# Index add on one core: one more staged batch, larger pieces for the copies, masks built on VectorE

## The chip, the cores and the metric

The kernel runs on one core of one Trainium2 chip. The metric is device time in microseconds (us) for one execution. Times are medians of several runs; the profile is of one execution, and its span (first to last instruction) is a little shorter than that execution's time.

## The reference

`x` has 32 batches of 512 rows of 256 floats. Every batch has 128 updates: an index (a row of this batch) and a source row of 256 floats. An index can occur several times in a batch.

```python
result = x.copy()
for b in range(32):
    for i in range(128):
        result[b, indices[b, i]] += source[b, i]
```

`x` and the result have 16.8 MB each, the source 4.2 MB.

## The kernel before

The kernel is a direct program: every instruction, semaphore and wait is written out, and each engine works through its own list in the order of the text. No planner moves anything.

There are two ways for a batch to reach the output.

**Direct batches** (26 of 32). The batch is copied from `x` to the output within DRAM (`copy`, L99, 512 KB, in rows of 4 KB). Beside this, the 128 rows that its updates name are gathered from `x` into a tile `got` by an indirect DMA of GpSimd (`gather`, L341). TensorE multiplies a 128 x 128 mask `same` (update i and update j have the same index) with the source rows, so that every update gets the sum of all updates to its row (L266). VectorE adds this to the gathered rows, for two batches at once (L278). An indirect DMA then scatters the rows over the copy (`scatter`, L359). Of several updates to one row only one may be written: VectorE multiplies `same` with the mask `before` and takes a maximum, and where an earlier update names the same row, the row number in `to_i` is pushed past the end, so that the transfer leaves this row out (L230 to L250). From the ninth direct batch on, the gather uses `to_i` as well and leaves these rows out too; the first eight use `row_i`, which is ready sooner.

**Staged batches** (`STAGED`, 6 of 32). The whole batch is loaded into SBUF (`load_x`, L112), 4 rows for each partition. VectorE compares the 512 row numbers in `place_f` with each update's index and so makes a mask `onehot` (L287), TensorE multiplies it with the source rows (L302), VectorE adds the result to the batch in two halves (L312), and SP stores it (L383).

The order around the change:

- SP issues, in one queue (q1 in the profile): the indices, the source for groups of four batches, the copies of batches 4 to 31, the loads of staged batches, and at the end the stores, each behind a wait for its last addition. ACT issues the copies of batches 0 to 3 in a queue of its own (q10), then clears some `got` tiles.
- GpSimd makes the constants (L129 to L157), waits for the row numbers, then issues all gathers and after them all scatters (q0). A gather with `to_i` waits for that group's masks. A scatter waits for its batch's copy, its sum and its masks.
- VectorE makes the row numbers and `place_f`, then the masks of groups 0 to 3. After that, for each group g: the sums of group g, the masks of group g + 4, and a staged batch of group g - 2 if there is one. The last staged batch comes at the end. TensorE follows the same order.

The loop that fixes this order:

```python
for g in range(NG):
    sums(g)
    if g + MASKS_AHEAD < NG:
        pe_broadcast(g + MASKS_AHEAD)
        dve_masks(g + MASKS_AHEAD)
    waiting += [b for b in STAGED if b // GB == g - 2]
    if waiting:
        staged_batch(waiting.pop(0))
```

Of the kernel before, what the change touches and what calls it, by code (L numbers as in the profile page):

```python
# [7 lines left out]
P = 128  # L8


GB = 4
COPY_DESC = 4096
STAGED = (7, 11, 15, 19, 23, 27)
MASKS_AHEAD = 4
SKIP_FROM = 8

# [2 lines left out]
def kernel(  # L19
# [13 lines left out]
    B, S, D = x.shape  # L33
    _, NU = indices.shape
    CH = S // P
    assert NU == P and S % P == 0 and B % GB == 0
    NG = B // GB
    DIRECT = [b for b in range(B) if b not in STAGED]
    N_DIRECT = len(DIRECT)
    assert N_DIRECT % 2 == 0  # L40

    f32 = mybir.dt.float32
    i32 = mybir.dt.int32
    Alu = mybir.AluOpType
# [5 lines left out]
    sb = ctx.enter_context(tc.tile_pool(name="sb", bufs=1))  # L50
# [3 lines left out]
    idx_bt = sb.tile([B, NU], f32)  # L54
    ident = sb.tile([B, B], f32)
    base = sb.tile([P, B], i32)
    before = sb.tile([P, GB, P], f32)
    place = sb.tile([P, CH, P], i32)
    place_f = sb.tile([P, CH, P], f32)
    idx_f = sb.tile([P, B], f32)  # L60
    base_f = sb.tile([P, B], f32)
    row_f = sb.tile([P, B], f32)
    row_i = sb.tile([P, B], i32)
    dup = sb.tile([P, B], f32)
    to_i = sb.tile([P, B], i32)
    src = [sb.tile([P, GB, D], f32, name=f"src{g}") for g in range(NG)]
    got = [sb.tile([P, 2, D], f32, name=f"got{h}") for h in range(N_DIRECT // 2)]
    same = [sb.tile([P, GB, P], f32, name=f"same{g}") for g in range(NG)]
    earlier = [sb.tile([P, GB, P], f32, name=f"earlier{k}") for k in range(2)]
    staged = {b: sb.tile([P, CH, D], f32, name=f"staged{b}") for b in STAGED}  # L70
    onehot = {b: sb.tile([P, CH, P], f32, name=f"onehot{b}") for b in STAGED}
    N_ADD, N_SP = 3, 2
    idx_ps = pp.tile([P, B], f32, space=PSUM)
    bc = [pp.tile([P, GB, P], f32, space=PSUM, name=f"bc{k}") for k in range(2)]
    add = [pp.tile([P, 2, D], f32, space=PSUM, name=f"add{k}") for k in range(N_ADD)]
# [5 lines left out]
    s_got = {b: tc.alloc_semaphore(f"s_got{b}") for b in DIRECT}  # L81
    s_in = {b: tc.alloc_semaphore(f"s_in{b}") for b in STAGED}
    s_out = tc.alloc_semaphore("s_out")
    s_store = tc.alloc_semaphore("s_store")
    sems = {n: tc.alloc_semaphore(f"s_{n}") for n in ("pool", "dve", "pe", "act")}
    done = dict.fromkeys(sems, 0)

    def mark(name, ins):
        ins.then_inc(sems[name], 1)
        done[name] += 1  # L90
        return done[name]

    V, T, G = nc.vector, nc.tensor, nc.gpsimd

    with tc.tile_critical(no_gpsimd_drain=True):  # L95
# [2 lines left out]

        def copy(b):  # L99
            (nc.scalar if b < GB else nc.sync).dma_start(  # L100
                out=out[b].rearrange("(p c) d -> p (c d)", p=P),
                in_=x[b].rearrange("(p c) d -> p (c d)", p=P),
                max_dma_last_dim=COPY_DESC,
            ).then_inc(s_copy[b], 16)

        def load_src(g):
# [5 lines left out]
        def load_x(b):  # L112
            nc.sync.dma_start(  # L113
                out=staged[b][:, :, :], in_=x[b].rearrange("(j c) d -> j c d", c=CH)
            ).then_inc(s_in[b], 16)
# [3 lines left out]
        for g in range(NG):  # L119
            if g + 2 < NG:  # L120
                load_src(g + 2)
            for b in range(g * GB, (g + 1) * GB):
                if b in DIRECT:
                    copy(b)
                if b % GB == 1 and g * GB - 1 in STAGED:
                    load_x(g * GB - 1)


        m = mark("pool", G.memset(ident[:, :], 0.0))  # L129
# [4 lines left out]
                out=ident[:, :], in_=ident[:, :], compare_op=Alu.not_equal, fill=1.0,  # L134
                base=0, pattern=[[-1, B]], channel_multiplier=1,
# [2 lines left out]
        k_const = mark(  # L138
            "pool", G.iota(out=base[:, :], pattern=[[S, B]], base=0, channel_multiplier=0)  # L139
        )  # L140

        k_place = mark(
            "pool",
            G.iota(
                out=place[:, :, :], pattern=[[1, CH], [CH, P]], base=0, channel_multiplier=0
            ),
        )

        m = mark("pool", G.memset(before[:, :, :], 1.0))
        G.wait_ge(sems["pool"], m)  # L150
        k_before = mark(
            "pool",
            G.affine_select(  # L153
                out=before[:, :, :], in_=before[:, :, :], compare_op=Alu.is_gt, fill=0.0,
                base=0, pattern=[[0, GB], [-1, P]], channel_multiplier=1,
            ),
        )  # L157


        for h in range(SKIP_FROM // 2, N_DIRECT // 2):  # L160
            k_zero = mark("act", nc.scalar.memzero(got[h][:, :, :]))  # L161


        V.wait_ge(sems["pool"], k_const)
        mark("dve", V.tensor_copy(out=base_f[:, :], in_=base[:, :]))  # L165
        V.wait_ge(s_idx, 16)
        k = mark(
            "dve",
# [1 line left out]
                out=idx_bt[:, :],  # L170
                in_=idx_raw[:, :].rearrange("b (u w) -> b u w", w=2)[:, :, 0],
# [5 lines left out]
        V.wait_ge(sems["pe"], k)  # L177
        k_rows = mark(
            "dve",
            V.tensor_tensor(out=row_i[:, :], in0=idx_ps[:, :], in1=base_f[:, :], op=Alu.add),  # L180
        )
        m = mark("dve", V.tensor_copy(out=idx_f[:, :], in_=idx_ps[:, :]))
        V.wait_ge(sems["dve"], m)
        mark(
            "dve",
            V.tensor_tensor(out=row_f[:, :], in0=idx_f[:, :], in1=base_f[:, :], op=Alu.add),
        )
        V.wait_ge(sems["pool"], k_place)
        m = mark("dve", V.tensor_copy(out=place_f[:, :, :], in_=place[:, :, :]))
        V.wait_ge(sems["dve"], m)  # L190

        k_bc, k_same, k_to, k_sum, k_hot, k_spread = {}, {}, {}, {}, {}, {}
        k_staged = {}

# [17 lines left out]
        def dve_masks(g):  # L212

            gs = slice(g * GB, (g + 1) * GB)
            V.wait_ge(sems["pe"], k_bc[g])
            k_same[g] = mark(
                "dve",
                V.tensor_tensor(  # L218
                    out=same[g][:, :, :],
                    in0=bc[g % 2][:, :, :],  # L220
                    in1=idx_f[:, gs].unsqueeze(2).to_broadcast([P, GB, P]),
                    op=Alu.is_equal,
                ),
            )
            if g == 0:
                V.wait_ge(sems["pool"], k_before)
            V.wait_ge(sems["dve"], k_same[g])
            m = mark(
                "dve",
                V.tensor_tensor(  # L230
                    out=earlier[g % 2][:, :, :], in0=same[g][:, :, :],
                    in1=before[:, :, :], op=Alu.mult,
                ),
            )
            V.wait_ge(sems["dve"], m)
            m = mark(
                "dve",
                V.tensor_reduce(  # L238
                    out=dup[:, gs], in_=earlier[g % 2][:, :, :], op=Alu.max,
                    axis=mybir.AxisListType.X,  # L240
                ),
            )
            V.wait_ge(sems["dve"], m)

            k_to[g] = mark(
                "dve",
                V.scalar_tensor_tensor(  # L247
                    out=to_i[:, gs], in0=dup[:, gs], scalar=float(2 * B * S),
                    in1=row_f[:, gs], op0=Alu.mult, op1=Alu.add,
                ),  # L250
            )

        def sums(g):

            T.wait_ge(s_src[g], 16)
            T.wait_ge(sems["dve"], k_same[g])
            for b in range(g * GB, (g + 1) * GB):
                if b in STAGED:
                    continue
                n = DIRECT.index(b)  # L260
                h = n // 2
                if n % 2 == 0 and h >= N_ADD:
                    T.wait_ge(sems["dve"], k_sum[h - N_ADD])
                k = mark(
                    "pe",
                    T.matmul(  # L266
                        out=add[h % N_ADD][:, n % 2, :], lhsT=same[g][:, b % GB, :],
                        rhs=src[g][:, b % GB, :], start=True, stop=True,
                    ),
                )  # L270
                if n % 2 == 0:
                    continue
                V.wait_ge(sems["pe"], k)
                V.wait_ge(s_got[DIRECT[n - 1]], 16)
                V.wait_ge(s_got[b], 16)  # L275
                k_sum[h] = mark(
                    "dve",
                    V.tensor_tensor(  # L278
                        out=got[h][:, :, :], in0=got[h][:, :, :],
                        in1=add[h % N_ADD][:, :, :], op=Alu.add,  # L280
                    ),
                )

# [40 lines left out]
        for g in range(MASKS_AHEAD):  # L324
            pe_broadcast(g)
            dve_masks(g)
        waiting = []
# [8 lines that stand above are left out]
# [45 lines left out]
        for b in STAGED:  # L381
            nc.sync.wait_ge(sems["dve"], k_staged[b])
            nc.sync.dma_start(  # L383
                out=out[b].rearrange("(j c) d -> j c d", c=CH), in_=staged[b][:, :, :]
# [34 lines left out]
```

## Time and profile before

| | |
|---|---|
| runs | median 83.69 us (83.33 to 83.92, 3 runs) |
| profiled execution | 83.13 us, span 81.4 us |
| busy share of the span | PE 54%, DVE (VectorE) 47%, ACT 7%, POOL (GpSimd) 67% |
| moved by DMA | 30.33 MB, mean 373 GB/s |
| indirect transfers | 26 gathers, 26 scatters, 1.0 us of POOL each |
| granted TensorE clock | 0.816 of full speed |

A busy digit of 9 in a slice means 90% or more of that fortieth of the span. The queue table has packets, MB, and the time that their packets took as a share of 16 engines over the span; shares of one stretch can add up to more than 1, since records of an engine's packets overlap. "us to landing" is from a transfer's issue until its data have arrived. In the timeline a line has the start, the length, the engine, the line of the kernel, the operation with its tiles, and in brackets the idle time before it and what ended that.

### The profile page before, as it was taken

The numbers are of one execution on the slowest core, as the hardware profiler recorded it, in microseconds if no ns is written. First come the engines' busy times: TensorE is split into PE (matmuls) and PEld (weight loads), VectorE is DVE, ScalarE is ACT, GpSimd is POOL, SyncE is SP. The second block draws the span as 40 slices with busy tenths as digits, with TensorE's granted clock in tenths as the row PEclk, the third lists the DMA queues.
The fourth block names the chain that finished last, engine by engine and source line by source line (L and its number), as shares of the span: only waits on it lengthen the run. The fifth ranks groups of instructions, "written<-read, shape, count | busy, mean of one in ns | idle before, by whom it ended". The sixth has DMA issues, their size and how long they took to land.

```text
span 81.4 us, 653 instructions
## 1 busy us (share of the span) xinstructions
PE 44.2 (54%) x165; PEld 34.8 (43%) x165; DVE 38.1 (47%) x69; ACT 6.1 (7%) x10; POOL 54.5 (67%) x62
## 2 busy tenths in 40 slices
PE   0299999999870099939494007993591900000000
PEld 0299986877540078638282006781460700000000
DVE  1749999999799903653700291009408006000000
ACT  0299700000000000000000000000000000000000
POOL 4668777877878787878777787877878687740000
PEclk9999999999999755599999985559858998555555
DMA  0899999999999999999999999999999999999930
GB/s 0 282 275 387 385 380 390 361 416 416 397 397 417 414 392 417 419 415 387 405 408 418 394 416 418 420 414 418 416 415 421 386 423 418 417 416 418 385 133 0
DMA packets 12243, 30.33 MB, mean 373 GB/s; under 512 B 1584, under 2 KB 5725, under 8 KB 12240
## 3 DMA queue, kind: packets, MB, share of 16 engines
q1 hardware_dynamic: 9168, 22.06, 69.5%
q0 software_dynamic: 2496, 6.15, 19.5%
q10 hardware_dynamic: 576, 2.10, 6.6%
q8 instruction: 1, 0.02, 0.1%
q14 instruction: 2, 0.02, 0.0%
HBM read 24.41 MB, written 20.19 MB: 548 GB/s over the span
## 4 chain that ended last, share of the span: by engine, by line
SPq 47%; DMA 18%; issue 10%; POOL 9%; DVE 2%; POOLq 2%; DVEq 0%
SPq L100 30%; DMA staged<-in_x_dram 18%; SPq L107 10%; POOL out_dram L363 9%; SPq L113 6%; POOLq L378 2%; DVE staged L312 1%; DVE got L278 1%; SPq L97 0%; DVEq L275 0%; SPq L414 0%; DVEq L308 0%; SPq L95 0%
## 5 line engine op out<-in xcount | busy, mean ns | idle before, releaser
L363 POOL DMA_INDIRECT out_dram<-got,to_i x26 | 25.7, 987 | 7.9 <-issue 7.0
L302 PE MATMUL spread<-src,onehot 128*128 128x256 f32 x48 | 16.8, 512 | 16.9 <-DVE onehot L287 14.6
L349 POOL DMA_INDIRECT got<-in_x_dram,to_i x18 | 18.2, 1012 | 5.5 <-issue 3.4
L302 PEld LDWEIGHTS spread<-src,onehot 128*128 128x128 f32 x48 | 11.6, 254 | 21.4 <-issue 19.4
L312 DVE TENSOR_TENSOR staged<-staged,spread 128x512 f32<-128x512 f32 x12 | 7.8, 684 | 25.4 <-DMA staged<-in_x_dram 16.5
L266 PE MATMUL add<-src,same 128*128 128x256 f32 x52 | 16.7, 469 | 0.4 <-DVE got L278 0.4
L266 PEld LDWEIGHTS add<-src,same 128*128 128x128 f32 x52 | 12.3, 245 | 3.6 <-DVE got L278 0.8
L203 PE MATMUL bc<-idx_bt,ident 32*128 32x128 f32 x64 | 11.9, 354 | 0.0
L203 PEld LDWEIGHTS bc<-idx_bt,ident 32*128 32x128 f32 x64 | 10.9, 256 | 1.4 <-DVE earlier L230 0.3
L349 POOL DMA_INDIRECT got<-in_x_dram,row_i x8 | 8.4, 1047 | 3.1 <-issue 1.8
L278 DVE TENSOR_TENSOR got<-got,add 128x512 f32<-128x512 f32 x13 | 8.6, 683 | 1.3 <-PE add L266 0.9
L218 DVE TENSOR_TENSOR same<-bc,idx_f 128x512 f32<-128x512 f32 x8 | 5.5, 684 | 1.1 <-PE bc L203 1.1
L230 DVE TENSOR_TENSOR earlier<-same,before 128x512 f32<-128x512 f32 x8 | 5.5, 692 | 0.3
L238 DVE TENSOR_REDUCE dup<-earlier 128x4 f32<-128x512 f32 x8 | 5.5, 686 | 0.3
L161 ACT ACTIVATE got<-got 128x512 uint32<-128x512 uint32 x9 | 4.8, 615 | 0.0
L287 DVE TENSOR_SCALAR onehot<-place_f,idx_f 128x512 f32<-128x512 f32 x6 | 2.9, 487 | 0.0
L176 PE MATMUL idx_ps<-ident,idx_bt 32*128 32x32 f32 x1 | 0.3, 280 | 3.6 <-DVE idx_bt L169 3.6
L165 DVE CAST base_f<-base 128x32 f32<-128x32 int32 x1 | 1.0, 993 | 1.7 <-POOL base L139 1.7
L176 PEld LDWEIGHTS idx_ps<-ident,idx_bt 32*128 32x128 f32 x1 | 0.2, 178 | 3.6 <-POOL before L153 3.6
L161 ACT ACT_TABLE_LOAD x1 | 1.3, 1283 | 3.6 <-issue 3.6
L247 DVE SCALAR_TENSOR_TENSOR to_i<-dup,row_f 128x4 int32<-128x4 f32 x8 | 1.3, 162 | 0.3
L169 DVE CAST idx_bt<-idx_raw 32x128 f32<-32x128 int32 x1 | 0.7, 687 | 0.1
(14 smaller groups left out, 3.6 us busy)
## 6 DMA issues: line engine op xcount, KB each, us to landing
out_dram<-in_x_dram SPq DMA_DIRECT2D x22, 512.0 KB, 15.0
src<-in_source_dram SPq DMA_DIRECT2D x8, 512.0 KB, 13.8
staged<-in_x_dram SPq DMA_DIRECT2D x6, 512.0 KB, 15.1
out_dram<-staged SPq DMA_DIRECT2D x6, 512.0 KB, 17.6
out_dram<-in_x_dram ACTq DMA_DIRECT2D x4, 512.0 KB, 7.9
out_dram<-got,to_i POOLq DMA_INDIRECT x26, 5.8
got<-in_x_dram,to_i POOLq DMA_INDIRECT x18, 5.9
got<-in_x_dram,row_i POOLq DMA_INDIRECT x8, 6.3
```

Source lines behind the costliest of these rows:

```text
L100: (nc.scalar if b < GB else nc.sync).dma_start(out=out[b].rearrange("(p c) d -> p (c d)", p=P), in_=x[b].rearrange("(p c) d -> p (c d)", p=P),
L107: nc.sync.dma_start(out=src[g][:, :, :], in_=source[g * GB : (g + 1) * GB].rearrange("e u d -> u e d"),).then_inc(s_src[g], 16)
L161: k_zero = mark("act", nc.scalar.memzero(got[h][:, :, :]))
L203: T.matmul(out=bc[g % 2][:, e, :], lhsT=ident[:, b : b + 1].to_broadcast([B, P]), rhs=idx_bt[:, :], start=True, stop=True,),
L218: V.tensor_tensor(out=same[g][:, :, :], in0=bc[g % 2][:, :, :], in1=idx_f[:, gs].unsqueeze(2).to_broadcast([P, GB, P]), op=Alu.is_equal,),
L230: V.tensor_tensor(out=earlier[g % 2][:, :, :], in0=same[g][:, :, :], in1=before[:, :, :], op=Alu.mult,),
L266: T.matmul(out=add[h % N_ADD][:, n % 2, :], lhsT=same[g][:, b % GB, :], rhs=src[g][:, b % GB, :], start=True, stop=True,),
L278: V.tensor_tensor(out=got[h][:, :, :], in0=got[h][:, :, :], in1=add[h % N_ADD][:, :, :], op=Alu.add,),
L302: T.matmul(out=spread[n % N_SP][:, c, :], lhsT=onehot[b][:, 2 * half + c, :], rhs=src[b // GB][:, b % GB, :], start=True, stop=True,),
L312: V.tensor_tensor(out=rows, in0=rows, in1=spread[n % N_SP][:, :, :], op=Alu.add),
L349: G.indirect_dma_start(out=got[n // 2][:, n % 2, :], out_offset=None, in_=x_rows, in_offset=bass.IndirectOffsetOnAxis(ap=(to_i if skips el ...
L363: G.indirect_dma_start(out=out_rows, out_offset=bass.IndirectOffsetOnAxis(ap=to_i[:, b : b + 1], axis=0), in_=got[n // 2][:, n % 2, :], in ...
```

## The change

Batch 3 becomes a staged batch as well, so 25 direct batches stay. Since their number is now odd, the last is summed by itself. The copies within DRAM are described as 32 rows of 16 KB instead of 128 rows of 4 KB. GpSimd no longer makes the wide constants `place` and `before`; it makes a row of counts, `column` (128 wide), and a column of counts, `update`. VectorE makes `before` (now 128 x 128) by one comparison and `place_f` by four operations out of these. The mask product reads `before` repeated for the four batches of a group. `base_f` goes: the additions read the integer `base`.

```diff
-COPY_DESC = 4096
-STAGED = (7, 11, 15, 19, 23, 27)
+COPY_ROWS = 32
+STAGED = (3, 7, 11, 15, 19, 23, 27)
...
-                out=out[b].rearrange("(p c) d -> p (c d)", p=P),
-                in_=x[b].rearrange("(p c) d -> p (c d)", p=P),
-                max_dma_last_dim=COPY_DESC,
+                out=out[b].rearrange("(p c) d -> p (c d)", p=COPY_ROWS),
+                in_=x[b].rearrange("(p c) d -> p (c d)", p=COPY_ROWS),
+                max_dma_last_dim=4 * S * D // COPY_ROWS,
...
-        k_place = mark(
-            "pool",
-            G.iota(
-                out=place[:, :, :], pattern=[[1, CH], [CH, P]], base=0, channel_multiplier=0
-            ),
-        )
-
-        m = mark("pool", G.memset(before[:, :, :], 1.0))
-        G.wait_ge(sems["pool"], m)
-        k_before = mark(
-            "pool",
-            G.affine_select(
-                out=before[:, :, :], in_=before[:, :, :], compare_op=Alu.is_gt, fill=0.0,
-                base=0, pattern=[[0, GB], [-1, P]], channel_multiplier=1,
-            ),
-        )
+        mark(
+            "pool", G.iota(out=update[:, :], pattern=[[0, 1]], base=0, channel_multiplier=1)
+        )
+        k_column = mark(
+            "pool", G.iota(out=column[:, :], pattern=[[1, P]], base=0, channel_multiplier=0)
+        )
...
-        mark("dve", V.tensor_copy(out=base_f[:, :], in_=base[:, :]))
...
-        V.wait_ge(sems["pool"], k_place)
-        m = mark("dve", V.tensor_copy(out=place_f[:, :, :], in_=place[:, :, :]))
+        V.wait_ge(sems["pool"], k_column)
+        m = mark("dve", V.tensor_copy(out=update_f[:, :], in_=update[:, :]))
         V.wait_ge(sems["dve"], m)
+        mark(
+            "dve",
+            V.tensor_scalar(
+                out=before[:, :], in0=column[:, :], scalar1=update_f[:, :], scalar2=None,
+                op0=Alu.is_lt,
+            ),
+        )
+        for c in range(CH):
+            k_place = mark(
+                "dve",
+                V.tensor_scalar(
+                    out=place_f[:, c, :], in0=column[:, :], scalar1=float(CH),
+                    scalar2=float(c), op0=Alu.mult, op1=Alu.add,
+                ),
+            )
...
-            if g == 0:
-                V.wait_ge(sems["pool"], k_before)
-            V.wait_ge(sems["dve"], k_same[g])
+            V.wait_ge(sems["dve"], max(k_same[g], k_place))
...
-                    in1=before[:, :, :], op=Alu.mult,
+                    in1=before[:, :].unsqueeze(1).to_broadcast([P, GB, P]), op=Alu.mult,
...
-                if n % 2 == 0:
+                if n % 2 == 0 and n + 1 < N_DIRECT:
                     continue
```

Batch 3 belongs to group 0, so by the loop above its staged work stands behind the masks of group 6 and ahead of the sums of group 3; the other staged batches keep their places. Its load is issued between the copies of batches 5 and 6. ACT issues three copies instead of four.

More of the change, by code (lines that the diff above doesn't have):

```diff
@@ L39 @@
     N_DIRECT = len(DIRECT)
-    assert N_DIRECT % 2 == 0
+    N_PAIR = (N_DIRECT + 1) // 2
     f32 = mybir.dt.float32
@@ L56 @@
     base = sb.tile([P, B], i32)
-    before = sb.tile([P, GB, P], f32)
-    place = sb.tile([P, CH, P], i32)
+    column = sb.tile([P, P], i32)
+    update = sb.tile([P, 1], i32)
+    update_f = sb.tile([P, 1], f32)
+    before = sb.tile([P, P], f32)
     place_f = sb.tile([P, CH, P], f32)
     idx_f = sb.tile([P, B], f32)
-    base_f = sb.tile([P, B], f32)
     row_f = sb.tile([P, B], f32)
@@ L66 @@
     src = [sb.tile([P, GB, D], f32, name=f"src{g}") for g in range(NG)]
-    got = [sb.tile([P, 2, D], f32, name=f"got{h}") for h in range(N_DIRECT // 2)]
+    got = [sb.tile([P, 2, D], f32, name=f"got{h}") for h in range(N_PAIR)]
     same = [sb.tile([P, GB, P], f32, name=f"same{g}") for g in range(NG)]
@@ L140 @@
         )
-        k_place = mark(
-            "pool",
-            G.iota(
-                out=place[:, :, :], pattern=[[1, CH], [CH, P]], base=0, channel_multiplier=0
-            ),
-        )
-        m = mark("pool", G.memset(before[:, :, :], 1.0))
-        G.wait_ge(sems["pool"], m)
-        k_before = mark(
-            "pool",
-            G.affine_select(
-                out=before[:, :, :], in_=before[:, :, :], compare_op=Alu.is_gt, fill=0.0,
-                base=0, pattern=[[0, GB], [-1, P]], channel_multiplier=1,
-            ),
+        mark(
+            "pool", G.iota(out=update[:, :], pattern=[[0, 1]], base=0, channel_multiplier=1)
+        )
+        k_column = mark(
+            "pool", G.iota(out=column[:, :], pattern=[[1, P]], base=0, channel_multiplier=0)
         )
-        for h in range(SKIP_FROM // 2, N_DIRECT // 2):
+        for h in range(SKIP_FROM // 2, N_PAIR):
             k_zero = mark("act", nc.scalar.memzero(got[h][:, :, :]))
         V.wait_ge(sems["pool"], k_const)
-        mark("dve", V.tensor_copy(out=base_f[:, :], in_=base[:, :]))
         V.wait_ge(s_idx, 16)
@@ L179 @@
             "dve",
-            V.tensor_tensor(out=row_i[:, :], in0=idx_ps[:, :], in1=base_f[:, :], op=Alu.add),
+            V.tensor_tensor(out=row_i[:, :], in0=idx_ps[:, :], in1=base[:, :], op=Alu.add),
         )
@@ L185 @@
             "dve",
-            V.tensor_tensor(out=row_f[:, :], in0=idx_f[:, :], in1=base_f[:, :], op=Alu.add),
+            V.tensor_tensor(out=row_f[:, :], in0=idx_f[:, :], in1=base[:, :], op=Alu.add),
         )
-        V.wait_ge(sems["pool"], k_place)
-        m = mark("dve", V.tensor_copy(out=place_f[:, :, :], in_=place[:, :, :]))
+        V.wait_ge(sems["pool"], k_column)
+        m = mark("dve", V.tensor_copy(out=update_f[:, :], in_=update[:, :]))
         V.wait_ge(sems["dve"], m)
+        mark(
[13 more added lines that the diff above has]
+            )
         k_bc, k_same, k_to, k_sum, k_hot, k_spread = {}, {}, {}, {}, {}, {}
@@ L270, in sums @@
                 )
-                if n % 2 == 0:
+                if n % 2 == 0 and n + 1 < N_DIRECT:
                     continue
                 V.wait_ge(sems["pe"], k)
-                V.wait_ge(s_got[DIRECT[n - 1]], 16)
-                V.wait_ge(s_got[b], 16)
+                for i in range(2 * h, n + 1):
+                    V.wait_ge(s_got[DIRECT[i]], 16)
+                rows = got[h][:, : n % 2 + 1, :]
                 k_sum[h] = mark(
@@ L278, in sums @@
                     V.tensor_tensor(
-                        out=got[h][:, :, :], in0=got[h][:, :, :],
-                        in1=add[h % N_ADD][:, :, :], op=Alu.add,
+                        out=rows, in0=rows, in1=add[h % N_ADD][:, : n % 2 + 1, :], op=Alu.add
                     ),
```

## The prediction

> **What bounds the kernel now.** I read the page's slices first, then the queue table, the chain, and last the ends of the three streams that could finish the run.
>
> ```profile
> DMA  0899999999999999999999999999999999999930
> GB/s 0 282 275 387 385 380 390 361 416 416 397 397 417 414 392 417 419 415 387 405 408 418 394 416 418 420 414 418 416 415 421 386 423 418 417 416 418 385 133 0
> ...
> q1 hardware_dynamic: 9168, 22.06, 69.5%
> q0 software_dynamic: 2496, 6.15, 19.5%
> q10 hardware_dynamic: 576, 2.10, 6.6%
> ...
> SPq 47%; DMA 18%; issue 10%; POOL 9%; DVE 2%; POOLq 2%; DVEq 0%
> ```
>
> The 16 DMA engines are at 9 tenths or more from about 4 us to 77 us, while no compute engine is above 67% of the span. The rate then stands near 415 GB/s whatever the compute engines do. [...] The chain of waits names an order, but the amount is DMA work. The same in stretches (columns: stretch, length, busy us of PE, PEld, DVE, ACT, POOL, granted clock, DMA share, GB/s):
>
> ```profile
> 40.00:56.00 16.00, 9.68 (x30) 7.51 (x30) 4.24 (x8) 0.00 (x0) 12.09 (x13) 0.79 1.03 411
> 56.00:72.00 16.00, 5.39 (x16) 3.70 (x16) 4.80 (x9) 0.00 (x0) 12.34 (x13) 0.78 1.03 414
> 72.00:76.00 4.00, 0.00 (x0) 0.00 (x0) 0.00 (x0) 0.00 (x0) 0.20 (x1) 0.50 1.04 420
> ```
>
> Three streams end close together. The last store of a staged batch is issued at 69.11 and lands 10.5 us later, at about 79.5. The last scatter (L363, POOL) starts at 71.22 and lands 6.1 us later, at 77.3. SP's own waits say the same: from 69.4, the end of its last issue, 8.1 us until the scatters, then 2.0 for the stores:
>
> ```profile
> SPq L388 <- DMA out_dram<-got,to_i: 8.1, 1, 8.1
> ...
> SPq L95 <- DMA out_dram<-staged: 2.0, 1, 2.0
> ```
>
> The span is 81.4 and the profiled execution took 83.13, so 1.7 us lie outside and are untouched. 83.13 is 0.56 below the median of the runs, 83.69; I work out a difference on the profile and apply it to the median.
>
> **Pieces of 16 KB.** Nothing of this size is copied in the trace, but the trace keeps a record of every packet, and I read medians from these: 46 ns for 1 KB, 159 ns for 4 KB, and 309 ns for the two 8 KB fetches that ran between other work at 37 and 40 us. One line fits all three: 8.3 ns and 36.8 ns for each KB. It gives 611 ns for 16 KB, against 4 x 159 = 636. (Check: 4128 x 46 + 4352 x 159 ns of q1 are 882 us; the page has 69.5% of 16 x 81.4 = 905.) The change copies 25 batches in 32 pieces each, 2 for each engine: at 25 ns saved, 50 pieces give 1.25 us of each engine's time. But the DMA shares of 1.03 and 1.04 above mean that records overlap, so part of the 8.3 ns is hidden already. At the 420 GB/s of 72 to 76 us an engine starts a new 4 KB every 16 x 4096 / 420 = 156 ns; 4 x 156 - 611 = 13 ns, times 50 is 0.65. I take 0.8, nearer to the second, because a rate and not a record sets the end. On the other side nothing excludes a loss: q10, whose copies opened the run, has 6.6% of 16 x 81.4 us = 86 us for 512 copy pieces, 168 ns each instead of 159. Pieces that are 9 ns for each 4 KB slower cost 25 x 8 x 9 = 1.8 us. The only 16 KB packet (queue 8, an instruction fetch) has a record of 1125 ns, which would be 50 x 489 ns = 24 us more; it is one fetch on an engine that was busy with others, so I stay with the copies' rows and keep +1.8 as the end.
>
> [...]
>
> **The seventh staged batch.** Batch 3 loses its copy (8 x 159 ns = 1.27 us of each engine), one gather and one scatter; q0's 19.5% of 81.4 is 15.9 us for 52 such transfers, 0.305 each. It gains a load and a store, 8 x 159 ns each, 2.54. Sum: 2.54 - 1.27 - 0.61 = +0.66 us of work in the queue that bounds. POOL has 50 indirect transfers left instead of 52, each about 0.99 busy and 0.30 idle: 2.6 us less, on a stream that has 2.2 us to spare already.
>
> On VectorE the batch comes early, between the masks of groups 6 and 7. The trace shows what a staged batch does there (batch 7, behind the masks of group 7):
>
> ```profile
> 27.98 0.16 DVE L247 SCALAR_TENSOR_TENSOR to_i<-dup,row_f 128x4 int32<-128x4 f32 x1
> 28.06 0.48 DVE L287 TENSOR_SCALAR onehot<-place_f,idx_f 128x512 f32<-128x512 f32 x1
> 30.77 0.69 DVE L312 TENSOR_TENSOR staged<-staged,spread 128x512 f32<-128x512 f32 x1 [2.23 <-PE spread L302]
> 32.48 0.69 DVE L312 TENSOR_TENSOR staged<-staged,spread 128x512 f32<-128x512 f32 x1 [1.02 <-PE spread L302]
> 33.34 0.69 DVE L278 TENSOR_TENSOR got<-got,add 128x512 f32<-128x512 f32 x1 [0.17 <-PE add L266]
> ```
>
> That is 5.1 us, of which 3.25 are spent waiting for PE. Behind it now stand the sums of group 3 and the masks of group 7, and behind those masks the gathers of batches 28 to 31, on POOL. One sum less stands ahead of it, so I put it from 24.3 to 29.4, two sums with their waits to 31.7, and the masks to about 33.9 (now 28.1). POOL gets to the gather of batch 28 at 32.3, so it waits some 1.6 us, and the 2.6 us saved shrink to 1.0: last scatter at about 70.2, landing at 76.3. Load 3 is not awaited: it and what is ahead of it are about 6 MB, landed by 18 us. The last scatter also waits for copy 31: now that is issued at 51.9, lands 18.8 us later at 70.7, and 8.8 us of stores and scatters follow it; with one store more some 10.3 follow, so it lands near 69.1 and holds nothing up. [...] Store 3 goes first of the seven.
>
> **Constants.** POOL loses iota, memset and select of 512 columns (0.55, 0.51, 0.63) and gets two small iotas. Its first gather waits for the row numbers at 4.39, and these for the indices landing at 2.7, so nothing is gained; only the conversion of 0.99 that ended at 2.7 goes, and the index conversion behind it started at 2.77. VectorE gets six small instructions: by the rows of 0.19 (32 columns) and 0.48 (512) about 0.25 for 128, so 1.4 us for these in place of 0.42, with starts overlapping rather less. They lie in the 1.10 us in which the first mask waited for PE's broadcast. Bounds: 0, or up to 0.9 at the head of a chain that has 2 us of cover, if the indices' packets stand behind two large pieces of the first copy (2 x 0.45). The mask multiplied with a repeated row has no row of its own; I hold it at 0.69, the other 512-column operations; 0.1 more on each of 8 would be 0.8 on VectorE, not on the queue.
>
> **Sum.** -0.8 + 0.66 = -0.14 us: 83.0 for the profiled execution, **83.5** on the median.
>
> **Rivals.** *The copies gain all of it, and the opening too.* Slices 2 and 3 run at 282 and 275 GB/s, 4 us that lack some 1.3 us of transfer at 415. Fewer, larger pieces in the first copies, and one copy less on ACT's queue, could fill part of it. With 1.25 saved and 0.3 to 1.2 from the opening: -0.9 to -1.8, 81.9 to 82.8. For it: one straight line through three sizes. Against: the other opening transfers, four loads in 1 KB rows, stay.
>
> *The large pieces run slower, and the kernel with them.* Place: 25 copies on all 16 engines. Price: +0.66 for the batch, plus 0.2 to 1.8 for the pieces, 84.5 to 86.1. It decides from 4 ns above 636 for a piece. For it: q10's 168 ns, and that each copy reads and writes the same memory at once. Against: the 159 ns hold for loads, copies and stores alike. The same sum without any saving, as when pieces are cut into 4 KB again, is +0.66, 84.35, still no change.
>
> *POOL ends last.* If the masks of group 7 come not at 33.9 but beyond 36.9, or the scatters land over 3 us later than reckoned, the scatters pass the stores; each us beyond is a us more. If every packet of an indirect transfer (two with data and a marker on each engine) had to stand behind one piece of 611 ns instead of 159, that would be 1.4 us on the 5.9 us to landing. At 2 us beyond: 85.5.
>
> [...] The trace shows only 4 KB beside gathers (5.8 to 6.3 us to landing). [...]
>
> **Numbers.** Under 1% either way is about what a measurement of this kernel can't tell from no change. Forecast 0.45, its cases from -0.6 to +0.7 all within 1%; copies and opening 0.26; slower pieces 0.21; POOL last 0.08. Faster 0.26, same 0.45, slower 0.29. The range takes in most of the rivals' prices: 82.2 to 85.3; the forecast's own is 83.1 to 84.4.
>
> **What will show it.** Right: 800 packets of 16 KB in place of 3328 of 4 KB for the copies; DMA rate in 40 to 56 us up by 1 to 3% from 411; the last store landing within 0.7 us of 79.5 and the scatters before it; a wait of POOL for VectorE near 32 us. Wrong: a rate below 411 there, gathers landing after 8 us or more, or a scatter as the last to land.

## The result: 1.45% slower

The changed kernel takes 84.9 us (median; 84.21 to 85.41) where the kernel before takes 83.81 (83.33 to 84.22). The ratio, estimated from the single runs, is **1.0145, with an interval of 1.0096 to 1.0194** (the quotient of the two medians is 1.0130). The forecast was 83.5 us and no change. The time lies inside the range; the direction was not the one forecast. The profiled execution took 85.22 us, 2.09 more than the one of before, with a span of 83.4 in place of 81.4. The ratios here and below leave out every run more than 1.5% above the fastest of its kernel, which for the pair measured side by side at the end drops none of the 6 runs of the changed kernel and 4 of the 12 of its padded form; the medians of all their runs give 1.0119 and 1.0028 instead of 1.0138 and 1.0013.

The lines of the page that answer to those shown of before (slices, queues, chain):

```profile
DMA  0899999999999999999998989999989999999700
GB/s 5 302 286 407 362 333 392 429 365 434 374 434 368 437 365 428 385 438 401 401 423 339 458 364 431 443 395 428 464 365 436 407 400 408 419 423 408 291 37 0
...
q1 hardware_dynamic: 7344, 23.10, 70.9%
q0 software_dynamic: 2400, 5.92, 18.5%
q10 hardware_dynamic: 144, 1.57, 4.7%
...
SPq 44%; DMA 26%; POOL 8%; issue 7%; DVE 2%; POOLq 2%; DVEq 0%
```

The DMA engines are as full as before, and they move 30.63 MB in place of 30.33. q10 now shows 144 packets: 96 pieces of 16 KB and 48 markers; 704 more pieces are in q1. The rate in the stretches that I had named (the columns are those of the prediction):

```profile
40.00:56.00 16.00, 13.57 (x53) 10.29 (x51) 9.02 (x15) 0.00 (x0) 12.35 (x13) 0.90 1.02 409
56.00:72.00 16.00, 5.09 (x17) 3.46 (x16) 4.95 (x9) 0.00 (x0) 12.05 (x13) 0.74 1.01 415
72.00:76.00 4.00, 0.00 (x0) 0.00 (x0) 0.00 (x0) 0.00 (x0) 1.97 (x2) 0.50 1.03 420
```

409 where 411 stood, not 1 to 3% more. At the end of the run, SP's waits (for what, us in total, times, longest):

```profile
SPq L391 <- DMA out_dram<-got,to_i: 11.5, 1, 11.5
...
SPq L96 <- POOLq L96: 0.9, 1, 0.9
SPq L96 <- DMA out_dram<-staged: 0.7, 1, 0.7
```

And from the timeline, POOL's wait before the gather of batch 28:

```profile
30.54 0.99 POOL L352 DMA_INDIRECT got<-in_x_dram,to_i  x1 [0.30 <-issue]
36.90 0.99 POOL L352 DMA_INDIRECT got<-in_x_dram,to_i  x1 [5.36 <-DVE to_i L250]
```

SP is done with its issues at 68.4, has the scatters 11.5 us later, the last store 0.7 after these, and then waits 0.9 us for POOL, which it did not do before. What POOL does there is a drain, which stands in both kernels behind the last scatter; the answer for its line in the kernel before (length in ns, start in us):

```profile
L378 POOLq DRAIN  x1: 8927/8927/8927, 70.8 to 70.8; - x1
```

and in the changed kernel:

```profile
L381 POOLq DRAIN  x1: 12335/12335/12335, 69.7 to 69.7; - x1
```

Before, the drain ended at 70.8 + 8.9 = 79.7, where the stores landed too (79.6). Now it ends at 69.7 + 12.3 = 82.0, with the last store at 80.7. So in this execution POOL ended last, by 1.3 us, as the third rival had it. From this came the first theory (A): the batch's work ahead of the last masks holds up the gathers. The rival theory (B) was that the 16 KB pieces slow the transfers. The runs showed that neither is where most of the loss comes from.

### The profile page after: what moved, and what is told of

Same layout as the page of the kernel before. It is cut to its first block, busy times and chain, and to the rows that moved or that the text cites. A ratio compares the mean times of both kernels' runs of the same rounds, so it can differ in the third digit from the quotient of the medians.

```text
span 83.4 us, 671 instructions
## 1 busy us (share of the span) xinstructions
PE 49.8 (60%) x171; PEld 38.7 (46%) x171; DVE 40.1 (48%) x76; ACT 6.1 (7%) x10; POOL 51.3 (62%) x59
## 2 busy tenths in 40 slices
DMA packets 9891, 30.63 MB, mean 367 GB/s; under 512 B 1568, under 2 KB 5709, under 8 KB 9088
## 4 chain that ended last, share of the span: by engine, by line
SPq 44%; DMA 26%; POOL 8%; issue 7%; DVE 2%; POOLq 2%; DVEq 0%
SPq L101 35%; DMA staged<-in_x_dram 26%; POOL out_dram L366 8%; SPq L108 6%; SPq L114 3%; POOLq L381 2%; DVE staged L315 1%; DVE onehot L290 1%; SPq L98 0%; SPq L417 0%; DVEq L311 0%; SPq L96 0%
## 5 line engine op out<-in xcount | busy, mean ns | idle before, releaser
L305 PE MATMUL spread<-src,onehot 128*128 128x256 f32 x56 | 18.4, 487 | 13.2 <-issue 7.1
L352 POOL DMA_INDIRECT got<-in_x_dram,to_i x17 | 17.3, 1019 | 10.2 <-DVE to_i L250 6.0
L305 PEld LDWEIGHTS spread<-src,onehot 128*128 128x128 f32 x56 | 12.8, 240 | 17.8 <-issue 15.7
L269 PE MATMUL add<-src,same 128*128 128x256 f32 x50 | 19.0, 539 | 0.0
L315 DVE TENSOR_TENSOR staged<-staged,spread 128x512 f32<-128x512 f32 x14 | 9.3, 685 | 18.4 <-PE spread L305 9.3
L269 PEld LDWEIGHTS add<-src,same 128*128 128x128 f32 x50 | 13.4, 275 | 3.3 <-issue 0.7
L208 PEld LDWEIGHTS bc<-idx_bt,ident 32*128 32x128 f32 x64 | 12.4, 291 | 2.5 <-DVE to_i L250 1.3
L208 PE MATMUL bc<-idx_bt,ident 32*128 32x128 f32 x64 | 13.6, 390 | 0.0
L282 DVE TENSOR_TENSOR got<-got,add 128x512 f32<-128x512 f32 (+1 forms) x13 | 8.4, 664 | 2.3 <-PE add L269 2.3
L290 DVE TENSOR_SCALAR onehot<-place_f,idx_f 128x512 f32<-128x512 f32 x7 | 3.9, 553 | 0.0
```

The costliest lines, as they stand in the source:

```text
L208: T.matmul(out=bc[g % 2][:, e, :], lhsT=ident[:, b : b + 1].to_broadcast([B, P]), rhs=idx_bt[:, :], start=True, stop=True,),
L269: T.matmul(out=add[h % N_ADD][:, n % 2, :], lhsT=same[g][:, b % GB, :], rhs=src[g][:, b % GB, :], start=True, stop=True,),
L282: V.tensor_tensor(out=rows, in0=rows, in1=add[h % N_ADD][:, : n % 2 + 1, :], op=Alu.add),
L305: T.matmul(out=spread[n % N_SP][:, c, :], lhsT=onehot[b][:, 2 * half + c, :], rhs=src[b // GB][:, b % GB, :], start=True, stop=True,),
L315: V.tensor_tensor(out=rows, in0=rows, in1=spread[n % N_SP][:, :, :], op=Alu.add),
L352: G.indirect_dma_start(out=got[n // 2][:, n % 2, :], out_offset=None, in_=x_rows, in_offset=bass.IndirectOffsetOnAxis(ap=(to_i if skips el ...
```

## Experiments

All ratios are to the kernel before, measured beside it; the interval is in brackets.

**First set: which part of the change?** Six staged batches with the rest of the change:

```diff
-STAGED = (3, 7, 11, 15, 19, 23, 27)
+STAGED = (7, 11, 15, 19, 23, 27)
```

> The changed kernel with six staged batches as before (batch 3 is copied, gathered and scattered again; the 16 KB pieces and the masks by VectorE stay). Theory A (the end is set by POOL: the gathers of the last group wait for masks that now stand behind batch 3's staged work, and POOL's drain ends 2.5 us after its last scatter has landed): POOL's wait of 5.4 us for the masks of group 7 is gone, the last scatter starts near 70.7 instead of 73.3, and the ratio to the kernel before is 0.985 to 1.00. Theory B (the 16 KB pieces cost the time, by slower transfers): still 1.005 to 1.015, with the stores landing later than 79.5.

Measured: 1.0066 (1.0033 to 1.0098). POOL's long wait was gone, the last scatter started at 71.7, and still the kernel was slower than before. Theory A had at most 1.00.

The rows of 4 KB again, with seven batches:

```diff
-COPY_ROWS = 32
+COPY_ROWS = 128
```

> The changed kernel with 128 rows of 4 KB for the copies again (seven staged batches and the masks by VectorE stay). Theory A: POOL still waits 4 to 6 us for the masks of group 7, its drain ends last, ratio 1.01 to 1.02. Theory B: the loss goes with the pieces, only the +0.66 us of the seventh batch stays: ratio 1.00 to 1.01, stores last.

Measured: 1.0088 (1.0049 to 1.0127), POOL waiting 5.4 us. Its value lies in theory B's range and its interval reaches into A's; by its end (POOL's drain at 82.7, the last store in at 81.4, and SP again waiting 0.9 us for POOL) it is theory A's.

Batch 3's staged work behind the masks of group 7:

```diff
-            waiting += [b for b in STAGED if b // GB == g - 2]
+            waiting += [b for b in STAGED if max(b // GB, 1) == g - 2]
```

> The changed kernel with the staged work of batch 3 moved behind the masks of group 7 (the other staged batches each one place later, the last two at the end). No work is left out. Theory A: POOL waits under 1 us for masks, its last scatter starts near 68.5 and lands by 75, the stores end the run near 80.3, and the drain no longer adds 0.9 us: ratio 0.995 to 1.005. Theory B: ratio 1.01 to 1.02 as for the changed kernel, since the transfers are the same.

Measured: 1.0101 (1.0063 to 1.0139). POOL did not wait for masks, its drain ended at 80.0, before the last store at 81.0, and yet 1% was left. So the place of the work is not the main part.

The kernel before with pieces of 16 KB alone:

```diff
-                out=out[b].rearrange("(p c) d -> p (c d)", p=P),
-                in_=x[b].rearrange("(p c) d -> p (c d)", p=P),
-                max_dma_last_dim=COPY_DESC,
+                out=out[b].rearrange("(p c) d -> p (c d)", p=COPY_ROWS),
+                in_=x[b].rearrange("(p c) d -> p (c d)", p=COPY_ROWS),
+                max_dma_last_dim=4 * S * D // COPY_ROWS,
```

> The kernel before with 16 KB pieces and nothing else. Theory A: scatters end as before, the drain with them, so at most a few tenths are gained although the stores land earlier: ratio 0.99 to 1.002. Theory B: ratio 1.005 to 1.015, and the stores land later than 79.5.

Measured: 0.9981 (0.995 to 1.0012). Theory B fell. With the six-batch kernel this left the masks, which I had priced at nothing: same batches, same pieces, 0.9981 without the new masks and 1.0066 with them.

**A new theory: where the tiles lie.** The rates had a pattern. In 30 to 50 us, when TensorE and VectorE work beside the transfers, the kernels with the new masks moved 400 to 407 GB/s and those without 409 to 410; from 52 to 70 us they were alike (413 to 417, but for 404 in the one with 4 KB pieces and seven batches). The two stretches of the kernel before:

```profile
30.00:50.00 20.00, 11.94 (x42) 9.14 (x42) 8.35 (x14) 0.00 (x0) 15.42 (x16) 0.84 1.04 409
52.00:70.00 18.00, 9.15 (x27) 6.44 (x25) 5.84 (x10) 0.00 (x0) 13.73 (x15) 0.78 1.03 414
```

and of the changed one:

```profile
30.00:50.00 20.00, 15.50 (x52) 11.66 (x51) 10.77 (x18) 0.00 (x0) 11.34 (x12) 0.75 1.03 403
52.00:70.00 18.00, 8.74 (x32) 6.42 (x32) 6.93 (x12) 0.00 (x0) 13.73 (x15) 0.83 1.01 415
```

What the new masks change for the transfers is not work but addresses. The tiles stand in SBUF in the order in which the program names them. `place` and `base_f` are gone, `before` is smaller, and `column`, `update` and `update_f` are new (512 bytes for each partition, and twice 4, for which 32 are taken: `update` starts at byte 18816, `update_f` at 18848); so everything named behind them, from `src0` on, moved by 3136 bytes, from byte 25216 of a partition to 22080. The first is a multiple of 128, the second is 64 past one. These starts are the ones in the built programs; the traces keep no addresses. Theory C: this offset slows the transfers. Theory D: it is something else in the masks.

The padding that tests it leaves every operation as it is:

```diff
-    update = sb.tile([P, 1], i32)
+    update = sb.tile([P, 24], i32)
...
-            "pool", G.iota(out=update[:, :], pattern=[[0, 1]], base=0, channel_multiplier=1)
+            "pool", G.iota(out=update[:, 0:1], pattern=[[0, 1]], base=0, channel_multiplier=1)
...
-        m = mark("dve", V.tensor_copy(out=update_f[:, :], in_=update[:, :]))
+        m = mark("dve", V.tensor_copy(out=update_f[:, :], in_=update[:, 0:1]))
```

Three kernels for this were first run in a set in which the kernel before took 91.31 us: the masks alone took 91.92, six batches with padding 92.01, and the late batch 3 with padding 91.16. Their ranges are 2.5 to 5.7 us wide and tell nothing apart. What was expected of them:

> The kernel before with the masks made by VectorE and nothing else (six staged batches, 4 KB pieces). In the changed kernel the small tiles shift every later tile of SBUF by 64 bytes against multiples of 128: src0 starts at byte 22080, before at 25216. Theory C (this shift slows the transfers that touch SBUF while the engines read it): ratio 1.004 to 1.01, and the rate between 16 and 50 us is 0.2 MB below that of before. Theory D (masks on VectorE cost nothing, and six staged with pieces was slower for the pieces): ratio 0.997 to 1.002.

> The changed kernel with six staged batches, and the tile update 24 columns wide instead of 1 (only the first is used), so that all later tiles keep the offset that they had in the kernel before, 128 past a multiple of 256. Theory C: ratio 0.992 to 1.00, against 1.0066 without the padding. Theory D: 1.004 to 1.009, unchanged.

> Seven staged batches, 16 KB pieces, masks by VectorE, batch 3 behind the masks of group 7, and the tile update 24 columns wide. Theory C: 0.5 to 0.9% below the same kernel without the padding (1.0101), so 1.000 to 1.005. Theory D: 1.007 to 1.013.

In the same set ran the changed kernel without POOL's drain:

```diff
-        G.drain()
```

> The changed kernel without the drain of POOL behind the scatters; SP waits for the scatters' semaphore as before, so all results have landed. Theory A (drain sets the end, 2.5 us after the last scatter has landed): the span ends about 1.0 to 1.3 us after the last landing plus 1 us, 0.5 to 0.9 us sooner, ratio 1.003 to 1.010 against 1.0145. If the drain at the program's end then takes the same 2.5 us, the ratio stays at 1.0145.

It took 95.39 us, 4.1 above the kernel before in that set, of which the changed kernel's own loss (1.1 us in the result, not measured in this set) is a part. The drain at the program's end now did the work, and alone. The answer for that line (three drains of POOL; lengths in ns):

```profile
L416 POOLq DRAIN  x3: 40/177/4148, 87.3 to 92.3; - x3
```

The last packet of the stores ended at 86.6 and that of the scatters at 84.0, and the drain that began at 87.3 took 4.1 us more. So its work is not the landing alone, and begun early it ends sooner: 2.1 us behind the last scatter's arrival in the changed kernel (82.0, with the scatters in at 79.9). Taking it out is a loss, which neither outcome that I had written down allowed.

The same three kernels again, and the seventh batch alone:

> The kernel before with the masks made by VectorE and nothing else, measured again (the first time all kernels of the set, the kernel before too, were 9% slower). Theory C (the small tiles shift all later SBUF tiles by 64 bytes, and that slows the transfers): ratio 1.004 to 1.01. Theory D (the masks cost nothing): 0.997 to 1.002.

Measured: 1.0075 (1.0033 to 1.0116). Theory D had 1.002 at most.

> Six staged batches, 16 KB pieces, masks by VectorE, the tile update 24 columns wide so that later tiles keep the offsets of the kernel before; measured again. Theory C: 0.992 to 1.00, against 1.0066 without the padding. Theory D: 1.004 to 1.009.

Measured: 0.9973 (0.9932 to 1.0014), against 1.0066 without the padding.

> Seven staged batches with batch 3 behind the masks of group 7, 16 KB pieces, masks by VectorE, the tile update 24 columns wide; measured again. Theory C: 1.000 to 1.005, against 1.0101 without the padding. Theory D: 1.007 to 1.013.

Measured: 1.0001 (0.9959 to 1.0044), against 1.0101 without.

The kernel before with `STAGED = (3, 7, 11, 15, 19, 23, 27)` and the handling of an odd last batch:

> The kernel before with batch 3 staged as well, and nothing else (4 KB pieces, masks by GpSimd, SBUF offsets as before). Theory A (POOL's gathers wait behind the batch's work on VectorE): POOL waits 2 to 6 us before the gather of batch 28, its drain ends last, 1.004 to 1.012. If only the DMA work counted, +0.66 us and the stores last: 1.006 to 1.009, and POOL's drain ends before the last store.

Measured: 0.9995 (0.995 to 1.004), below both ranges. POOL waited 3.79 us before the gather of batch 28, and no cost is seen: the drain ended at 80.5, the last store was in at 81.6. The seventh batch is free to within 0.4%, with its place as it is.

**The offset by itself.** The kernel before with a wider tile `to_i`, by 64 and by 128 bytes, and nothing else:

```diff
-    to_i = sb.tile([P, B], i32)
+    to_i = sb.tile([P, B + 16], i32)
```

> The kernel before, with 64 more bytes behind the tile to_i, so that src0 and every tile behind it start 64 bytes past a multiple of 128; no instruction differs. If the offset alone costs what the masks seemed to cost: ratio 1.005 to 1.01, and some 0.2 MB less moved between 16 and 50 us. If the masks' instructions were the cause: 0.997 to 1.003.

Measured: 1.0019 (0.9976 to 1.0062). The value lies in the range written down for the other cause, the masks' instructions, and the interval reaches into both, so this run doesn't show that the offset costs time in the kernel before. The rate in 30 to 50 us fell to 403 GB/s, as in the other kernels with the offset.

> The kernel before, with 128 more bytes behind to_i, so that src0 and every later tile start at a multiple of 256 (now 128 past one). If a multiple of 128 is all that matters: 0.997 to 1.003. If multiples of 256 are better still: 0.985 to 0.996.

Measured: 0.9979 (0.9933 to 1.0026), 409 GB/s. A multiple of 256 gains nothing that can be measured over one of 128. Over 16 to 50 us, the stretch that the expectations name, the kernels split by their rates as well (407 to 410 GB/s against 396 to 404), but for this profile, which has 397 there.

> The changed kernel with the tile update 24 columns wide, so that later tiles keep the offsets of the kernel before. If the offset costs 0.7 to 0.9% and the place of batch 3's work 0.4%: ratio 1.003 to 1.008, POOL still waiting 3 to 5 us and its drain ending last. If the place costs nothing: 0.997 to 1.002.

Measured: 0.996 (0.9903 to 1.0018). This is the changed kernel with the padding alone, and no loss can be told from zero. POOL still waited (2.74 us), but its drain ended at 79.5, before the last store at 80.8.

Six batches, where only the source tiles have the offset of before and the tiles behind them (gathered rows, masks, staged batches) are 64 past a multiple of 128:

```diff
     src = [sb.tile([P, GB, D], f32, name=f"src{g}") for g in range(NG)]
+    gap = sb.tile([P, 16], f32)
     got = [sb.tile([P, 2, D], f32, name=f"got{h}") for h in range(N_PAIR)]
```

> Six staged batches, 16 KB pieces, masks by VectorE; the source tiles at the offsets of the kernel before, the tiles behind them (gathered rows, masks, staged batches) 64 bytes past a multiple of 128. If the loads of the source, in rows of 1 KB, are what the offset slows: 0.994 to 1.001, as with all tiles padded (0.997). If gathers, scatters and staged transfers are: 1.004 to 1.009, as without padding (1.0066).

Measured: 1.0064 (1.0023 to 1.0104) at 408 GB/s. The time says that the tiles behind the source are the ones that matter, the rate of the one profile says that the source does. It stays open.

**Side by side.** The changed kernel and its padded form on one chip:

> The changed kernel itself, on the same chip as h2, so that the two differ in nothing but the offset of the tiles behind update (64 against 128 past a multiple of 256). If the offset is most of the loss: 1.009 to 1.017, about 0.8% or more above h2. If not: within 0.4% of h2.

Measured: **1.0138 (1.0086 to 1.019)**.

> The changed kernel with the tile update 24 columns wide, measured again beside the changed kernel. If the offset is most of the loss: 0.996 to 1.006. If the place of batch 3's work is, too: at least 1.004, with POOL's drain ending last.

Measured: **1.0013 (0.9965 to 1.006)**. The intervals do not meet, and the two programs differ in nothing but the width of one tile and what it moves. The stretch of 16 to 50 us of the changed kernel:

```profile
16.00:50.00 34.00, 21.44 (x88) 16.51 (x86) 20.51 (x37) 0.00 (x0) 25.35 (x25) 0.90 1.03 404
```

and of the padded one:

```profile
16.00:50.00 34.00, 24.50 (x91) 18.78 (x90) 21.19 (x37) 0.00 (x0) 24.25 (x25) 0.85 1.02 408
```

The DMA engines are fully busy in both (a share of 1.03 and 1.02) and move 404 and 408 GB/s. Over 34 us these 4 GB/s are 0.14 MB, a third of a microsecond; the ratios differ by 1.05 us. So these single profiles show only part of the difference. They could not show all of it: the two profiled executions took 84.76 us (the fastest of the changed kernel) and 84.89 (the ninth of the padded one's twelve). By the medians of the packets' records no size is slower by more than 1 ns (in q1: 1 KB 46 ns in both, 4 KB 159 in both, 16 KB 614 and 613); means differ, among them that of the 1 KB packets, which load the source (51.0 and 48.9).

In this second profile of the changed kernel POOL is not last any more. SP's waits there:

```profile
SPq L391 <- DMA out_dram<-got,to_i: 8.0, 1, 8.0
SPq L96 <- DMA out_dram<-staged: 2.9, 1, 2.9
```

and POOL's drain:

```profile
L381 POOLq DRAIN  x1: 8887/8887/8887, 71.5 to 71.5; - x1
```

The drain ends at 80.4, and the stores come last, 2.9 us after the scatters. The kernel is 1.4% slower all the same. That POOL ended last in the first profile goes with TensorE's pace in that execution. The same work, a group's six products, in the first profile:

```profile
15.15 2.93 PE L269 MATMUL add<-src,same 128*128 128x256 f32 x6
```

and in this one:

```profile
14.73 1.56 PE L269 MATMUL add<-src,same 128*128 128x256 f32 x6
```

TensorE kept the slower pace until 22.8 us in the first profile and until about 14 in this one, with a granted clock of 1.00 from 13 to 23 us in both; the masks of group 7 came late, and POOL with them. The one other profile in which SP is seen to wait for POOL at the end, that with 4 KB pieces, had the slower pace until 23.6 us. With seven batches in the kernel before it lasted until 23.0, POOL waited 3.79 us, and the stores still came last. What sets the moment, no run shows.

All kernels outside the set at 91 us together, by the offset of their tiles:

| kernel | offset past a multiple of 128 | ratio | GB/s, 30 to 50 us |
|---|---|---|---|
| before | 0 | 1 | 409 |
| before, 16 KB pieces | 0 | 0.9981 | 410 |
| before, seven batches | 0 | 0.9995 | 408 |
| before, tiles moved by 128 | 0 | 0.9979 | 409 |
| six batches, pieces, masks, padded | 0 | 0.9973 | 410 |
| changed, batch 3 late, padded | 0 | 1.0001 | 411 |
| changed, padded | 0 | 0.996, 1.0013 | 413, 412 |
| changed | 64 | 1.0145, 1.0138 | 403, 406 |
| changed, batch 3 late | 64 | 1.0101 | 407 |
| changed, 4 KB pieces | 64 | 1.0088 | 400 |
| six batches, pieces, masks | 64 | 1.0066 | 404 |
| before, masks by VectorE | 64 | 1.0075 | 403 |
| before, tiles moved by 64 | 64 | 1.0019 | 403 |
| six batches, pieces, masks, source at 0 | 0 and 64 | 1.0064 | 408 |

The rates are of one profiled execution each, the ratios of several runs. Every kernel with the tiles on a multiple of 128 has an interval that holds 1. Of those with the offset, all but one have an interval above 1; the one is the kernel before with nothing but the offset. Three pairs differ by the padding alone: 1.0066 and 0.9973, 1.0101 and 1.0001, 1.0138 and 1.0013; only the last was measured in one set.

No version was shown to be faster than the kernel before: the padded kernels come to 0.996 to 1.0013 with intervals that hold 1.

## Why the prediction was wrong

- **What bounds the kernel** was right: the DMA engines are full, in every kernel (a share of 1.03 to 1.05 in 30 to 50 us in all 16 profiles outside the set at 91 us), and what counts is what they move and at which rate. That the offset acts through the rate is argued, not shown: the rates seen in one pair of profiles make up a third of the loss.
- **Constants** is the step that failed. I priced each instruction that went or came, rightly at nothing (six batches with pieces: 0.9981 with the old masks, 0.9973 with the new ones and padding), and did not ask what else a tile does when it goes or comes: it moves all tiles named behind it. That is worth 1.25% here (1.0138 against 1.0013; 0.9% by the medians of all runs), about 1 us. In the kernel before the same offset cost nothing that could be measured (1.0019, 0.9976 to 1.0062), so what else of the changed kernel it needs is not known. The trace of before could not show the price, but the addresses could be reckoned from the tiles' sizes, and the step should have held them as an unknown with two bounds.
- **The range**: that 84.9 us lies in 82.2 to 85.3 is luck. The upper part was there for slower pieces and for POOL ending last, and neither is where the loss came from.
- **Pieces of 16 KB**: the length of the packet was right, the sum was not reached. (The line's 36.8 ns are for each 1000 bytes; for 1024 it is 37.7, with the same 611 ns at 16,384 bytes.) The records of the pieces in the changed kernel have a minimum of 611 ns and a median of 614 in q1, where 611 was forecast. The 0.8 us taken for it came to 0.16 (0.9981 of 83.8; the interval is -0.4 to +0.1). Part of it is in the opening: the 128 pieces that ACT issues have a mean of 697 ns in the kernel with pieces alone, 86 ns over the line, or 0.7 us of each engine for its 8, where the 4 KB packets there were 0.25 over. That the rest lies in waits of single packets is likely, but only read from profiles of single executions.
- **The seventh batch**: +0.66 us was forecast, 0.9995 (-0.4 to +0.3 us) measured. The term was too large; why is not known. POOL's wait was right in kind, and in size where TensorE's slower pace ended early: the gather of batch 28 was forecast for 33.9, and was at 33.05 in the second profile of the changed kernel and at 34.06 in that of the padded one beside it, but at 36.90 in the first profile of the changed kernel.
- **The slack of POOL** was read wrongly. I gave the scatters 2.2 us to spare, from their landing to the last store's. But POOL's drain stands behind them: in all 16 profiles outside the set at 91 us it ended 2.1 to 2.2 us after SP had the last scatter (2.17 in the eight with 52 indirect transfers, 2.08 or 2.09 in the eight with 50). So the two streams ended within 0.1 us of each other in the kernel before, and the third rival's point was over 2 us nearer than I put it. In 14 of the 16 the drain ended between 1.3 us before and 0.5 us after the last store was in; in the other two, the first profile of the changed kernel and the one with 4 KB pieces, it ended 1.3 us after.
- **Rivals and chances**: "the large pieces run slower" fell. "POOL ends last" was seen, by 1.3 us, in two profiles and is not the main cause: the loss stays where POOL does not end last (1.0101 with the late batch 3) and goes with the padding. The cause was in none of them.
- **Indirect transfers beside the pieces**: with pieces in the kernel before, gathers land after 7.7 and 6.8 us (before: 6.3 and 5.9) and scatters after 6.5 (5.8), so 0.7 to 1.4 more. That is up to the 1.4 worked out for three packets that each stand behind one piece; that they do stand so, no run shows. It cost nothing that shows in the ratio (0.9981).

The offset itself is only partly explained. Tiles at 128 past a multiple of 256 (the kernel before) and at a multiple (0.9979, 0.9933 to 1.0026) can't be told apart, and only 64 came out slower. Which access is slowed, and by what, stays open.

## What to carry to other kernels

A tile that is added, removed or resized moves every tile allocated behind it. Where the DMA engines are full, reckon the start of the transferred tiles; here a start on a multiple of 128 bytes, by padding a small tile, took a 1.4% loss away in the changed kernel, though the kernel before lost nothing measurable off it. A difference of 1% that no instruction explains is worth that test before any theory on the instructions. Where two streams end together, look for what stands behind the last transfer on its engine (here a drain) before calling one of them slack. One profile shows one execution: who ended last differed between two profiles of the same kernel.

## What the runs showed of the hardware

- Tiles that start 64 bytes past a multiple of 128: 400 to 408 GB/s in 30 to 50 us against 408 to 413, with the DMA engines full in both (a share of 1.03 to 1.05), and 0.9 to 1.25% of the changed kernel's time side by side; in the kernel before no cost was measured (1.0019, 0.9976 to 1.0062). From 52 to 70 us, with less compute beside the transfers, no such difference is seen: 409 to 417 in both groups, with one exception in each (404 and 396).
- A packet of 16 KB takes 611 ns at the least; with 46, 159 and 309 ns for 1, 4 and 8 KB this is one straight line of 8.3 ns and 37.7 ns for each 1024 bytes.
- POOL's drain behind the scatters ended 2.1 to 2.2 us after SP had the last of them, in 16 profiles. Begun only after everything had landed, at the program's end, it took 4.1 us in one profile of the set at 91 us.
- TensorE took 2.93 us for six products of L269 in one execution and 1.56 in another at the same place of the same kernel, with a granted clock of 1.00 in both; the slower pace at the start ended between 13 and 24 us, at different times in the 16 profiles.
